# The second matrix products of two MLPs with seven block products in place of eight, in a float32 decoder trunk

## The chip, the cores and the metric

The kernel runs on one core of a Trainium2 chip. The metric is the device time of one execution in microseconds. The time before is the median of three runs, 1213.51 us (1211.22 to 1214.91). The trace comes from one further execution, recorded by the hardware profiler. Line numbers (L297) are those of the kernel before.

## The reference

The reference is a decoder trunk of two layers on 512 tokens of width 1024, in float32. Layer 1 mixes tokens with differential attention, layer 2 with an mLSTM. After each mixer stands an MLP with a squared ReLU, and both parts are added to the residual stream. A last RMSNorm ends it.

```python
def sqrelu_mlp(h, w1, w2):
    return jnp.square(jax.nn.relu(h @ w1)) @ w2
...
        h = h + mix.astype(h.dtype)
        h = h + sqrelu_mlp(rmsnorm(h, mlp_norm[layer]), mlp_w1[layer], mlp_w2[layer]).astype(h.dtype)
    return rmsnorm(h, final_norm)
```

`w1` is 1024 x 4096 and `w2` is 4096 x 1024, so that each MLP has two products of 512 x 1024 x 4096 multiply-adds. The change touches the second one, with `w2`.

## The kernel before

**Layout.** The residual stream lies transposed in SBUF: `h[k]` (k = 0 to 7) holds 128 channels by 512 tokens, two of them to a tile `h2`. A matmul takes a 128 x 128 tile of weights as its stationary operand and streams up to 512 token columns.

**Three matmuls for one product.** Float32 precision comes from splitting each operand into a high part in the format float32r and a low remainder (`split`, L423: ScalarE copies into the high part, VectorE subtracts to get the low one). A product is then high x high, high x low and low x high, three matmuls that accumulate in one PSUM bank (`mm3`, L296 to L299).

**Weights.** The host packs all weights in the order in which they are used, in units of 128 x 1024 numbers, 512 KB (`_plan`, L80). `issue` (L263) loads a unit through SyncE's DMA queue and splits it on ScalarE (L281) and VectorE (L282) into `whi` and `wlo`; raw, high and low tiles are rings of three. `unit` (L291) hands out the next unit and first issues those two ahead of it. A unit feeds 8 tiles times 3 matmuls.

**The MLP** (`mlp`, L733). The 4096 inner columns are done in two halves of 16 column tiles. For each tile of a half `ntile_mm` multiplies all 1024 input channels, ScalarE takes the ReLU out of PSUM, VectorE squares it, and a split makes `uh` and `ul` (L747 to L758). Then for each of the 8 output tiles two units of `w2` accumulate over the half's 16 inner tiles in one bank; VectorE multiplies by the squared token scale `rs2` (the RMSNorm's factor, pulled out behind the ReLU) and adds to `h[n]` (L766, L767). In the second half each finished `h[n]` becomes an operand of the next mixer at once (`operand`, L405), with its squares summed over tiles on GpSimd (`square_in`, L414 to L420). This sum over channels gives the next RMSNorm's factor by a matmul with a constant matrix (`token_scale`, `sums`).

**The tail** (`finish`, L1032). In layer 2 the last output tile is worked off in two halves of 256 tokens, 48 narrow matmuls each (L1084 to L1086), so that the final RMSNorm and the stores of the first half run beside the matmuls of the second. After the first half's matmuls `early_sums` (L1043) adds the squares of the first seven tiles into the statistic.

**What sets the order.** TensorE runs in the order in which the program is written (`manual_schedule`, L165). Small steps are woven into it by a count of matmul groups: `after(n, fn)` calls `fn` after n further ticks; `T_MLP`, `T_FIN` and others are such distances. For VectorE, ScalarE, GpSimd and the DMA queues the framework's planner orders the instructions when the program is built; each engine then runs its own queue in that order and waits on semaphores.

## Time and profile before

| | |
|---|---|
| median of three runs | 1213.51 us (1211.22 to 1214.91) |
| the profiled execution | 1211.02 us, span 1209.2 us |
| instructions | 14346, of them 5610 matmuls |
| mean granted TensorE clock | 0.992 |
| DMA | 111.15 MB moved, 92 GB/s on average |
| weight loads | 188 of 512 KB and 6 smaller or wider ones |

A page of the profile gives, for each engine, the time in which it was busy and its number of instructions. PE is TensorE's matmuls and PEld its weight loads, which overlap; DVE is VectorE, ACT ScalarE, POOL GpSimd, SP SyncE. Matmuls are pipelined: a row's duration is longer than the distance to the next one, so the cost of a matmul in a stream is read from the distance between starts. A row of a group names line, engine, operation, what is written and read, the shape and the count, then the busy time, the mean of one in ns, and the engine's idle time just before with what ended it. A row of the timeline gives start and duration in us, and in brackets the idle time before and its releaser. A line can be that of a helper: every ScalarE activation has L230.

### The profile page before, as it was taken

The numbers are of one execution on the slowest core, as the hardware profiler recorded it, in microseconds if no ns is written. First come the engines' busy times: TensorE is split into PE (matmuls) and PEld (weight loads), VectorE is DVE, ScalarE is ACT, GpSimd is POOL, SyncE is SP. The second block draws the span as 40 slices with busy tenths as digits, with TensorE's granted clock in tenths as the row PEclk, the third lists the DMA queues.
The fourth block names the chain that finished last, engine by engine and source line by source line (L and its number), as shares of the span: only waits on it lengthen the run. The fifth ranks groups of instructions, "written<-read, shape, count | busy, mean of one in ns | idle before, by whom it ended". The sixth has DMA issues, their size and how long they took to land.

```text
span 1209.2 us, 14346 instructions
## 1 busy us (share of the span) xinstructions
PE 1175.9 (97%) x5610; PEld 975.0 (81%) x5610; DVE 684.5 (57%) x1063; ACT 524.2 (43%) x845; POOL 168.7 (14%) x157
## 2 busy tenths in 40 slices
PE   8899999999999999999999899999999999999996
PEld 5778888888888888888887789878888888888885
DVE  6789897575433344434469857666544333444444
ACT  5567776454331223433344546655433122433221
POOL 4432332130000000001101312213000000000011
PEclk9999999999999999999999999999999999999998
DMA  6622222222322223232321221222232323222222
GB/s 197 197 70 70 79 79 71 76 99 87 103 89 90 102 87 104 87 103 89 98 93 64 89 69 53 70 87 87 92 100 87 104 88 103 90 91 101 87 70 70
DMA packets 33123, 111.15 MB, mean 92 GB/s; under 512 B 3967, under 2 KB 6034, under 8 KB 33056
## 3 DMA queue, kind: packets, MB, share of 16 engines
q1 hardware_dynamic: 30288, 103.38, 25.9%
q0 software_dynamic: 1648, 5.29, 1.6%
q10 hardware_dynamic: 1120, 1.57, 0.4%
q8 instruction: 44, 0.72, 0.2%
q14 instruction: 23, 0.19, 0.1%
HBM read 108.11 MB, written 4.74 MB: 93 GB/s over the span
## 4 chain that ended last, share of the span: by engine, by line
PE 84%; DVE 8%; ACT 3%; DMA 2%; issue 2%; POOL 1%; DVEq 0%; SPq 0%; ACTq 0%; POOLq 0%
PE bank L298 24%; PE bank L299 24%; PE bank L297 24%; PE bank L330 1%; PE bank L329 1%; PE bank L331 1%; DVE wlo_wlo L282 1%; DMA raw_raw<-wgt 1%; DVE tmp_tmp L827 1%; PE bank L623 1%; PE bank L624 1%; ACT kh_kh L230 1%; PE bank L656 1%; ACT whi_whi L230 1%; DVE e_e L643 0%
## 5 line engine op out<-in xcount | busy, mean ns | idle before, releaser
L282 DVE TENSOR_TENSOR wlo_wlo<-raw_raw,whi_whi 128x1024 fp32r<-128x1024 f32 (+1 forms) x194 | 243.1, 1253 | 269.2 <-ACT whi_whi L230 268.9
L230 ACT ACTIVATE whi_whi<-raw_raw 128x1024 fp32r<-128x1024 f32 (+1 forms) x194 | 203.6, 1049 | 403.4 <-PE bank L298 358.9
L299 PE MATMUL bank<-x_xh,wlo_wlo 128*128 128x512 f32 x768 | 306.0, 398 | 1.1 <-DVE wlo_wlo L282 1.1
L298 PE MATMUL bank<-x_xl,whi_whi 128*128 128x512 f32 x768 | 305.0, 397 | 1.1 <-DVE x_xl L409 1.1
L297 PE MATMUL bank<-x_xh,whi_whi 128*128 128x512 f32 x768 | 303.3, 395 | 2.0 <-ACT whi_whi L230 1.5
L299 PE MATMUL bank<-u_uh,wlo_wlo 128*128 128x512 f32 x496 | 197.1, 397 | 0.0
L298 PE MATMUL bank<-u_ul,whi_whi 128*128 128x512 f32 x496 | 196.3, 396 | 0.0
L297 PE MATMUL bank<-u_uh,whi_whi 128*128 128x512 f32 x496 | 193.7, 391 | 0.0
L297 PEld LDWEIGHTS bank<-x_xh,whi_whi 128*128 128x128 f32 x768 | 146.9, 191 | 35.3 <-ACT whi_whi L230 2.2
L298 PEld LDWEIGHTS bank<-x_xl,whi_whi 128*128 128x128 f32 x768 | 145.0, 189 | 34.3 <-DVE x_xl L409 1.8
L299 PEld LDWEIGHTS bank<-x_xh,wlo_wlo 128*128 128x128 f32 x768 | 144.9, 189 | 34.1 <-DVE wlo_wlo L282 2.1
L420 POOL TENSOR_TENSOR acc_acc<-acc_acc,tmp_tmp 128x512 f32<-128x512 f32 x34 | 53.6, 1576 | 717.8 <-ACT tmp_tmp L230 717.1
L297 PEld LDWEIGHTS bank<-u_uh,whi_whi 128*128 128x128 f32 x496 | 94.6, 191 | 22.0
L298 PEld LDWEIGHTS bank<-u_ul,whi_whi 128*128 128x128 f32 x496 | 93.1, 188 | 22.1
L299 PEld LDWEIGHTS bank<-u_uh,wlo_wlo 128*128 128x128 f32 x496 | 93.1, 188 | 20.2
L766 DVE TENSOR_TENSOR tmp_tmp<-bank,rs_rs 128x512 f32<-128x512 f32 x31 | 21.4, 692 | 107.1 <-PE bank L299 107.1
L230 ACT ACTIVATE u_uh<-tmp_tmp 128x512 fp32r<-128x512 f32 x64 | 40.4, 632 | 79.1 <-DVE tmp_tmp L754 78.9
L329 PE MATMUL bank<-whi_whi,x_xh 128*128 128x256 f32 (+1 forms) x256 | 72.7, 284 | 0.0
L330 PE MATMUL bank<-wlo_wlo,x_xh 128*128 128x256 f32 (+1 forms) x256 | 72.1, 282 | 0.0
L331 PE MATMUL bank<-whi_whi,x_xl 128*128 128x256 f32 (+1 forms) x256 | 72.0, 281 | 0.0
L424 DVE TENSOR_TENSOR u_ul<-tmp_tmp,u_uh 128x512 fp32r<-128x512 f32 x64 | 44.3, 692 | 39.1 <-ACT u_uh L230 39.1
L329 PEld LDWEIGHTS bank<-whi_whi,x_xh 128*128 128x128 f32 x256 | 48.3, 189 | 0.5
(242 smaller groups left out, 1493.3 us busy)
## 6 DMA issues: line engine op xcount, KB each, us to landing
raw_raw<-wgt SPq DMA_DIRECT2D x188, 512.0 KB, 3.5
skew<-frd POOLq DMA_DIRECT2D x8, 320.0 KB, 6.7
bias_bias<-skew POOLq DMA_DIRECT2D x8, 256.0 KB, 3.1
outT<-h SPq DMA_DIRECT2D x6, 256.0 KB, 2.3
raw_raw<-wgt SPq DMA_DIRECT2D x2, 528.0 KB, 3.6
h<-xT ACTq DMA_DIRECT2D x4, 256.0 KB, 6.8
raw_raw<-wgt SPq DMA_DIRECT2D x4, 256.0 KB, 8.7
h<-xT SPq DMA_DIRECT2D x4, 256.0 KB, 6.4
```

The costliest lines, as they stand in the source:

```text
L230: ins = nc.scalar.activation(out, x, func, **kw)
L282: vec.tensor_tensor(lo[:, c], raw[:, c], asf(hi[:, c]), op=ALU.subtract)
L297: mm(ps, whi, x[0], start=first, stop=False)
L298: mm(ps, whi, x[1], start=False, stop=False)
L299: mm(ps, wlo, x[0], start=False, stop=last)
L329: mm(ps, xh, hi[:, c], start=k == 0, stop=False)
L330: mm(ps, xh, lo[:, c], start=False, stop=False)
L331: mm(ps, xl, hi[:, c], start=False, stop=k == KT - 1)
L420: pool.tensor_tensor(acc, acc, s, op=ALU.add)
L424: (eng or vec).tensor_tensor(lo, src, asf(hi), op=ALU.subtract)
L623: mm(ps[m][:, o : o + n], q2[m][:, qs], kh[m][:, :n], start=True, stop=False)
L766: vec.tensor_tensor(y, p, rs2, op=ALU.mult)
```

## The change

The inner columns are now done in four quarters of 8 tiles. In each quarter the second product is cut into blocks: two output tiles (256 columns of `w2`) by the quarter's 1024 inner columns by 512 tokens. The weights of a block are the four pieces A11, A12, A21, A22 (512 inner columns by 128 output columns each), the hidden activations four pieces B (512 inner columns by 256 tokens each). Eight products of pieces become seven, with sums of pieces as operands:

- On the weights' side S1 = A21 + A22, S3 = A21 - A11, S2 = S1 - A11 and S4 = A12 - S2 are made on VectorE. A block's weights come as four pieces of work: `first` (two loads, and the split of A11 with A12), `sums1` (S1, S3), `half` (A22 alone) and `sums2` (S2, S4). Each MLP brings one more raw, high and low tile and a separate tile for `half`.
- On the activations' side `hidden` makes three differences of B's pieces on VectorE, and keeps seven 256-column blocks for each inner tile, all split into high and low. There are five such slots. The token scale is now applied ahead of the square, in one VectorE instruction with the ReLU, and ScalarE squares.
- `down` runs the seven products, each 4 inner tiles x 3 matmuls of 256 columns, into four PSUM banks, and assembles the block's result from them on VectorE in four additions (after ScalarE has copied the first product out of PSUM).
- In the first three quarters the assembled block is added to the residual by a DMA with an add, issued by GpSimd; in the last one by VectorE, for two tiles at once. Then follow `operand` or `square_in` for both.
- One pair of column tiles of the next quarter's first product is placed ahead of a quarter's four blocks. In the last quarter the first block takes three of the inner tiles through all products and then the fourth.
- In layer 2 the very last block stays a plain product. `finish` now works off two output tiles over one quarter, and `early_sums` follows the first of its four groups of 24 matmuls.
- The tiles of the weight rings are picked by a list of free ones, and the GpSimd DMAs' descriptor space is set to 4096.

The diff, cut to what the text speaks of:

```diff
--- before.py
+++ after.py
@@ -80,6 +80,7 @@
...
+    def pair(m, q, p, kind="pair"):
+        for n in (2 * p, 2 * p + 1):
+            units.append((m, [(8 * q + 2 * s + i, n * P, P) for i in range(2) for s in range(4)]))
+        if kind == "pair":
+            pairs.add(len(units) - 2)
...
+        for what, q, i in MLP_ORDER:
+            if what == "up":
+                for n in (8 * q + 2 * i, 8 * q + 2 * i + 1):
+                    if n >= 4:
+                        ntile(m1, n * P)
+            else:
+                pair(m2, q, i, "plain" if last and (q, i) == (3, 3) else "pair")
...
+MLP_ORDER = [("up", 0, i) for i in range(4)]
+for _q in range(4):
+    if _q < 3:
+        MLP_ORDER.append(("up", _q + 1, 0))
+    MLP_ORDER += [("down", _q, i) for i in range(4)]
+    if _q < 3:
+        MLP_ORDER += [("up", _q + 1, i) for i in range(1, 4)]
+PLAN, PAIRS = _plan()
+PIECES = []
+for _u in range(len(PLAN)):
+    if _u in PAIRS:
+        PIECES += [(kind, _u) for kind in ("first", "sums1", "half", "sums2")]
+    elif _u - 1 not in PAIRS:
+        PIECES.append(("unit", _u))
...
+    def fits():
+        kind, u = PIECES[state["next"]]
+        mine = PLAN[u][0][0] == "w"
+        def some(tag):
+            return sum((mine or all(t is not e for e in extra.get(tag, ()))) and id(t) not in live for t in ring[tag])
+        if kind == "half":
+            return id(extra["half"][0]) not in live
+        if not some("whi") or not some("wlo"):
+            return False
+        return kind not in ("unit", "first") or some("raw") > (kind == "first")
     def issue():
...
+        i = state["next"]
+        kind, u = PIECES[i]
+        assert fits()
         state["next"] += 1
...
+        if kind == "first":
+            extra["pair"] = room("raw", u), room("raw", u)
+            for i, r in enumerate(extra["pair"]):
+                nc.sync.dma_start(r[:, :1024], source(u + i))
+        r1, r2 = extra["pair"]
+        a11, a12, a21, a22 = r1[:, :512], r1[:, 512:1024], r2[:, :512], r2[:, 512:1024]
+        sums_of = extra["sums"]
+        s1, s3, s2, s4 = (sums_of[:, i * 512 : (i + 1) * 512] for i in range(4))
+        if kind == "first":
+            split(r1[:, :1024], hi[:, :1024], lo[:, :1024])
+        elif kind == "half":
+            split(a22, hi, lo)
+        elif kind == "sums1":
+            vec.tensor_tensor(s1, a21, a22, op=ALU.add)
+            vec.tensor_tensor(s3, a21, a11, op=ALU.subtract)
+            split(sums_of[:, :1024], hi[:, :1024], lo[:, :1024])
+        else:
+            vec.tensor_tensor(s2, s1, a11, op=ALU.subtract)
+            vec.tensor_tensor(s4, a12, s2, op=ALU.subtract)
+            split(sums_of[:, 1024:], hi[:, :1024], lo[:, :1024])
+            free(r1, r2)
...
         return ps
+    chains = sp.tile([P, 4 * T], F32, name="chains")
     def chain(tag):
-        return sp.tile([P, T], F32, tag=tag, name=nm(tag), bufs=1)
+        i = ("nx", "ny", "na", "sq").index(tag)
+        return chains[:, i * T : (i + 1) * T]
...
-            up = Buffers(tc, st, name="up", bufs=32)
+            up = Buffers(tc, st, name="up", bufs=1)
+            B = 256
+            slots = [tuple(up.tile([P, 7 * B], F32R, name=f"u{s}{i}") for s in "hl") for i in range(5)]
+            for tag in ("raw", "whi", "wlo"):
+                t = up.tile([P, 1024], F32 if tag == "raw" else F32R, name=f"{tag}x")
+                extra[tag] = [t]
+                ring[tag].insert(0, t)
+            extra["half"] = [up.tile([P, 512], F32R, name=f"half{s}") for s in "hl"]
+            extra["sums"] = up.tile([P, 2048], F32, name="wsums")
+            work = up.tile([P, 8 * B], F32, name="work")
+            F = chains
+            fb = F.rearrange("p (b c) -> p b c", c=B)
+            wb = work.rearrange("p (b c) -> p b c", c=B)
...
-            rs2 = scale_tile("rs2")
-            def scale():
-                rs = tmp()
-                token_scale(acc, rs)
-                act(rs2, rs, AF.Square)
-            after(T_MLP, scale)
-            for half in range(2):
...
+            def hidden(p, j, q, i):
+                m = tmp()
+                vec.scalar_tensor_tensor(m, p, 0.0, rs, op0=ALU.max, op1=ALU.mult)
+                act(fb[:, 2:8:5] if j == 0 else fb[:, 0:2], m.rearrange("p (a c) -> p a c", a=2), AF.Square)
+                if j == 0:
+                    return
+                b12 = fb[:, 7:8].to_broadcast([P, 2, B])
+                vec.tensor_tensor(fb[:, 3:5], b12, fb[:, 1:3], op=ALU.subtract)
+                vec.tensor_tensor(fb[:, 5], fb[:, 2], fb[:, 3], op=ALU.subtract)
+                vec.tensor_tensor(fb[:, 6], fb[:, 0], fb[:, 5], op=ALU.subtract)
+                hi, lo = slots[(4 * q + i) % 5]
+                split(F[:, : 7 * B], hi, lo)
+                if finish is not None and q == 3:
+                    split(F[:, 7 * B :], *spare(i))
+            PRODUCTS = (("P1", "A11", 2), ("P2", "A12", 0), ("P4", "A22", 6), ("P5", "S1", 4), ("P7", "S3", 3),
+                        ("P6", "S2", 5), ("P3", "S4", 1))
+            def down(q, i):
+                for z in list(held):
+                    done_with(z)
+                own = [take() for _ in range(4)]
+                ahead(own[-1])
+                forms = {}
+                for z, names_ in zip(own, (("A11", "A12"), ("S1", "S3"), ("A22",), ("S2", "S4"))):
+                    for j, name in enumerate(names_):
+                        forms[name] = [t[:, j * 512 : (j + 1) * 512] for t in ready[z]]
+                def more():
+                    if state["next"] <= min(own[-1] + 4, len(PIECES) - 1) and fits():
+                        issue()
+                more()
+                d, a, c, b = (bank() for _ in range(4))
...
+                       "P3": c[:, :B], "P4": c[:, B:]}
+                late = q == 3 and i == 0
+                for ks in ((0, 1, 2), (3,)) if late else ((0, 1, 2, 3),):
+                    for name, w, block in PRODUCTS:
+                        hi, lo = forms[w]
+                        for k in ks:
+                            uh, ul = slots[(4 * q + k) % 5]
+                            t = slice(block * B, (block + 1) * B)
+                            n = slice(k * P, (k + 1) * P)
+                            first = k == 0 and not (late and name in ("P7", "P6", "P3"))
+                            mm(out[name], hi[:, n], uh[:, t], start=first, stop=False, skip_group_check=late)
+                            mm(out[name], hi[:, n], ul[:, t], start=False, stop=False, skip_group_check=late)
+                            mm(out[name], lo[:, n], uh[:, t], start=False, stop=k == 3, skip_group_check=late)
+                            tick()
+                        if ks[-1] == 3:
+                            if name == "P1":
+                                act(wb[:, 7], d[:, :B], AF.Copy)
+                            last = {"P2": 0, "P7": 1, "P4": 2, "P3": 3}.get(name)
+                            if last is not None:
+                                done_with(own[last])
+                                more()
+                def two(z):
+                    return z.rearrange("p (a c) -> p a c", a=2)
+                vec.tensor_tensor(wb[:, 0:5:4], two(a), wb[:, 7:8].to_broadcast([P, 2, B]), op=ALU.add)
+                vec.tensor_tensor(wb[:, 5:7], two(b), wb[:, 4:5].to_broadcast([P, 2, B]), op=ALU.add)
+                vec.tensor_tensor(wb[:, 1:3], two(c), wb[:, 5:7], op=ALU.add)
+                vec.tensor_tensor(wb[:, 3], b[:, :B], wb[:, 6], op=ALU.add)
+                hp_ = h2[i].rearrange("p a t -> p (a t)")
+                if q < 3:
+                    nc.gpsimd.dma_start(hp_, work[:, : 4 * B], accum_op=ALU.add)
+                    return
+                vec.tensor_tensor(hp_, hp_, work[:, : 4 * B], op=ALU.add)
+                for n in (2 * i, 2 * i + 1):
+                    if g0 is not None:
                         nxt.append(operand(n, g0, nacc))
-                    elif half == 1:
+                    else:
                         if n == 0:
-                            facc = acc_tile()
-                            finish.acc = facc
+                            finish.acc = acc_tile()
                         square_in(n, finish.acc)
+            after(T_MLP, lambda: token_scale(acc, rs))
...
+            for what, q, i in MLP_ORDER:
+                if what == "up":
+                    for j in range(2):
+                        n = 2 * i + j
+                        hidden(ps[n] if q == 0 and n < 4 else ntile_mm(x), j, q, i)
+                elif finish is not None and (q, i) == (3, 3):
+                    def operands(k, t):
+                        s, j = k % 4, k // 4
+                        hi, lo = slots[(12 + s) % 5]
+                        block = (2, 7)[t] if j == 0 else t
+                        if block == 7:
+                            return spare(s)
+                        w = slice(block * B, (block + 1) * B)
...
-    def finish(hid, rs2):
-        last = KT - 1
+    def finish(operands):
+        pair = (KT - 2, KT - 1)
         acc = finish.acc
...
                 mm(s[:, :H], ones_d, sh[:, c], start=True, stop=False)
                 mm(s[:, :H], ones_d, sl[:, c], start=False, stop=False)
...
-        def tail(c, stat, wait):
-            y = tmp()[:, :H]
-            vec.tensor_tensor(y, part[:, c], rs2[:, c], op=ALU.mult)
-            vec.tensor_tensor(h[last][:, c], h[last][:, c], y, op=ALU.add)
-            s = tmp()[:, :H]
-            act(s, h[last][:, c], AF.Square)
-            vec.tensor_scalar(h[last][:, c], h[last][:, c], col(C_FN + last), -0.5, op0=ALU.mult, op1=ALU.mult)
-            after(wait, lambda: scaled(c, stat, s))
...
+        def scaled(c, stat, ss):
+            for s in ss:
+                mm(stat[:, :H], ones_df, s, start=False, stop=s is ss[-1])
             x, y, a = (chain(t)[:, :H] for t in ("nx", "ny", "na"))
...
-                    mm(part[:, c], hi[:, w], a, start=u + k == 0, stop=False)
-                    mm(part[:, c], hi[:, w], b, start=False, stop=False)
-                    mm(part[:, c], lo[:, w], a, start=False, stop=u == 1 and k == KT - 1)
+                    a, b = operands(k, i)
+                    mm(part[j][:, c], hi[:, w], a, start=k == 0, stop=False)
+                    mm(part[j][:, c], hi[:, w], b, start=False, stop=False)
+                    mm(part[j][:, c], lo[:, w], a, start=False, stop=k == KT - 1)
                     tick()
+                tail(n, c, ss[j])
+                if i == 0 and j == 0:
+                    early_sums()
             if i == 0:
-                early_sums()
-                tail(c, stat[i], T_FIN)
+                after(T_FIN, lambda c=c, ss=ss: scaled(c, stat[0], ss))
             else:
-                tail(c, stat[i], 0)
...
-    nc = _bacc.Bacc("TRN2", target_bir_lowering=False, num_devices=1)
+    nc = _bacc.Bacc("TRN2", target_bir_lowering=False, num_devices=1, dynamic_dma_scratch_size=4096)
     aps = {}
```

More of the change, by code (lines that the diff above doesn't have):

```diff
@@ L296, in mm3, with ahead, done_with, take @@
+    used = iter(range(len(PIECES)))
+    held = []
+    def ahead(i):
+        while state["next"] <= min(i, len(PIECES) - 1):
+            issue()
+    def done_with(i):
+        held.remove(i)
+        free(*ready.pop(i))
+    def take():
+        i = next(used)
+        held.append(i)
+        return i
+    def unit(n=2, keep=False):
+        if not keep:
+            for i in list(held):
+                done_with(i)
+        i = take()
+        ahead(i + n)
+        return ready[i]
     def mm3(ps, whi, wlo, x, first, last):
@@ L746, in mlp @@
[L746 to L768 removed]
+            rs = scale_tile("rs2")
@@ L775, in mlp @@
+            for tag in ("raw", "whi", "wlo"):
+                (t,) = extra.pop(tag)
+                ring[tag] = [r for r in ring[tag] if r is not t]
             return nxt, nacc
```

140 lines of the change are left out of this document (72 added, 68 removed).

## The prediction

> **What bounds the kernel now.** I read the page's busy table first, then its busy slices, then busy time by stage, then the groups by shape inside one stage, then single rows at the two places where the change shortens a cover.
>
> ```profile
> span 1209.2 us, 14346 instructions
> PE 1175.9 (97%) x5610; PEld 975.0 (81%) x5610; DVE 684.5 (57%) x1063; ACT 524.2 (43%) x845; POOL 168.7 (14%) x157
> PE 84%; DVE 8%; ACT 3%; DMA 2%; issue 2%; POOL 1%; DVEq 0%; SPq 0%; ACTq 0%; POOLq 0%
> ```
>
> TensorE is busy for 97% of the span and carries 84% of the chain that ended last. The profiled execution took 1211.02 us, 1.8 more than its span, and lies 2.5 us under the median of the three runs (1213.51). Those runs spread over 0.3%, which is about what a measurement of this kernel can tell from no change.
>
> ```profile
> core 0: us, PE busy (x) PEld busy (x) DVE busy (x) ACT busy (x) POOL busy (x), PEclk, DMA share, GB/s
> 826.00:1184.40 358.40, 358.40 (x1546) 291.39 (x1545) 152.53 (x173) 113.75 (x145) 13.66 (x9) 1.00 0.28 92
> 1184.40:1209.20 24.80, 13.44 (x105) 12.55 (x103) 13.38 (x22) 4.71 (x10) 5.08 (x3) 0.84 0.25 85
> ```
>
> ```profile
> 1184.42 0.28 PE L1084 MATMUL bank<-u_uh,whi_whi 128*128 128x256 f32 x1
> ...
> 1190.12 0.28 PE L1046 MATMUL bank<-sh_sh,ones_d 128*128 128x256 f32 x1
> ```
>
> The first row is the second layer's MLP up to its last column tile: TensorE is never idle there (358.40 of 358.40 us) at full granted clock, while VectorE is busy 43% and ScalarE 32%. So in this stage a matmul removed is time removed, as long as nobody else becomes late. Two prices follow. A 512-column matmul: 358.40 us / 1546 = 0.2318 us. A 256-column matmul: the last two rows bracket the 48 matmuls of lines 1084 to 1086 on the first token half, in the same pattern the change uses (high x high, high x low, low x high), so 5.70 us / 48 = 0.1188 us. Two narrow ones cost 0.2375 against 0.2318 for a wide one, 2.5% more per column.
>
> **Term 1, TensorE's work.** One block of the second product is two column tiles by one quarter (8 row tiles) of the inner columns. Before: 2 x 8 x 3 = 48 wide matmuls, 11.13 us. After: 7 products x 4 row tiles x 3 = 84 narrow ones, 9.98 us. Layer 1 has 16 blocks: 768 x 0.2318 = 178.0 becomes 1344 x 0.1188 = 159.7, or -18.3. Layer 2 has 720 wide and 96 narrow ones (166.9 + 11.4 = 178.3); it gets 15 blocks and a last plain one of 96 narrow matmuls, 1356 x 0.1188 = 161.1, or -17.2. Together **-35.5 us**. The first product's matmuls stay as they are.
>
> Here the Trainium skill speaks against the change: "TensorE: Matmul & The Clock Gate", section "LDWEIGHTS (loading the stationary operand)", puts a weight load at columns / 1.2 ns, so about 107 ns for 128 columns, and its Part 3 says that loads overlap running matmuls only in another row group. By that, 107 + 107 = 214 ns per narrow matmul, the block would grow to 84 x 0.214 = 18.0 us. The narrow matmuls of this trace start 0.1188 us apart, each with a load of its own, so the trace does not agree.
>
> **Term 2, VectorE and ScalarE in the blocks.** What is added has no price on TensorE unless it makes weights or banks late. The groups by shape in a stretch of second products give the prices:
>
> ```profile
> L282 DVE TENSOR_TENSOR wlo_wlo<-raw_raw,whi_whi 128x1024 fp32r<-128x1024 f32 x17 | 20.8, 1222 | 35.7 <-ACT whi_whi L230 35.7
> L298 PEld LDWEIGHTS bank<-u_ul,whi_whi 128*128 128x128 f32 x102 | 19.2, 188 | 4.5
> L230 ACT ACTIVATE whi_whi<-raw_raw 128x1024 fp32r<-128x1024 f32 x16 | 17.0, 1061 | 67.1 <-PE bank L298 67.1
> L766 DVE TENSOR_TENSOR tmp_tmp<-bank,rs_rs 128x512 f32<-128x512 f32 x7 | 4.8, 692 | 24.3 <-PE bank L299 24.3
> L754 DVE TENSOR_TENSOR tmp_tmp<-tmp_tmp 128x512 f32<-128x512 f32 x2 | 1.4, 685 | 0.0
> L230 ACT ACTIVATE u_uh<-tmp_tmp 128x512 fp32r<-128x512 f32 x2 | 1.3, 632 | 2.8 <-DVE tmp_tmp L754 2.8
> ```
>
> ```profile
> 1190.32 0.42 DVE L1054 TENSOR_TENSOR tmp_tmp<-bank,rs_rs 128x256 f32<-128x256 f32 x1 [0.51 <-PE bank L1086]
> ```
>
> VectorE per second-product block: three 1024-wide splits (A11 with A12, S1 with S3, S2 with S4) 3 x 1.222, the half split of A22 0.69, four 512-wide sums 4 x 0.685, the assembly of four results 3 x 0.692 + 0.42: **9.6 us in 9.98**. Before it was 2 x 1.222 plus two evictions. ScalarE: 3 x 1.061 + 0.632 + 0.42 = 4.2 us. VectorE per first-product block (two column tiles, 11.13 us on TensorE): two splits 2.44, two evictions 1.38, three subtractions 0.685 + 2 x 0.42, and a 1792-wide split, by width 1.75 x 1.222 = 2.14: 7.5 us. So VectorE goes from idle half of the time to 17.1 of 21.1 us, yet stays under TensorE in both kinds of block.
>
> Its queue is not free of gaps: the low half of each split waits for ScalarE's high half, and those of the sums can't start before the sums. The written order would leave it idle about 1.1 us at each of the two sum pieces, 11.8 us a block. But every piece of block b+1 is written while block b runs. Reckoned from the start of b: the first split ends by 4 us and is due at 10; the first sums end by 8, due at 14.3 (three of seven products into b+1); the second sums, whose tile product five frees at 7.1, end by 10 to 12, due at 17. So each has 5 to 7 us in hand, and TensorE doesn't see the gaps. I take 0 for each of the eight quads (four quarters in two layers); the bound is 2 us a quad, and below 0 there is nothing, since TensorE had no idle time here to give back.
>
> The 24 adds into the residual that go through GpSimd as accumulating DMAs lie off every chain until the third quarter's sum is read, some 40 us later; but each reads `work`, which the next block's assembly overwrites after its sixth product, 8.55 us into the block, or 7.3 us after the issue at about 1.2.
>
> ```profile
> raw_raw<-wgt SPq DMA_DIRECT2D x188, 512.0 KB, 3.5
> skew<-frd POOLq DMA_DIRECT2D x8, 320.0 KB, 6.7
> ```
>
> The trace has no accumulating DMA. Its nearest rows are 3.5 us for a plain 512 KB load and 6.7 for GpSimd's copies issued eight at a time; 5 to 7 us fits into 7.3, so I take 0.
>
> The Trainium skill, "DMA: Bandwidth & Descriptors", section "Anatomy of one DMA — SWDGE (gpsimd) path", gives about 2.0 us + bytes/436e3 for a plain transfer from GpSimd, by estimate 3.2 us for 512 KB; no run here shows an accumulating one, and the sum would be the same.
>
> **Term 3, the tail of the second layer.** Here an exposed chain appears. `finish` multiplies the square sums of the finished tiles into `stat` (lines 1046 and 1047) between its matmuls. The chain for it before:
>
> ```profile
> 1184.62 0.69 DVE L766 TENSOR_TENSOR tmp_tmp<-bank,rs_rs 128x512 f32<-128x512 f32 x1 [3.42 <-PE bank L299]
> ...
> 1186.13 0.63 ACT L230 ACTIVATE tmp_tmp<-h 128x512 f32<-128x512 f32 x1 [6.19 <-DVE h L767]
> 1188.46 0.63 ACT L230 ACTIVATE sh_sh<-acc_acc 128x512 fp32r<-128x512 f32 x1 [1.69 <-POOL acc_acc L420]
> ...
> 1186.90 1.52 POOL L420 TENSOR_TENSOR acc_acc<-acc_acc,tmp_tmp 128x512 f32<-128x512 f32 x1 [9.69 <-ACT tmp_tmp L230]
> ...
> 1189.12 0.69 DVE L424 TENSOR_TENSOR sl_sl<-acc_acc,sh_sh 128x512 fp32r<-128x512 f32 x1 [1.84 <-ACT sh_sh L230]
> ```
>
> It ended at 1189.81, 5.4 us after the last wide matmul's successor at 1184.42, and TensorE came to line 1046 at 1190.12: hidden by 48 narrow matmuls. After the change two column tiles end together, and `early_sums` stands behind only the first 24 matmuls, 2.85 us. The chain from the end of block (3,2): 0.2, the one assembly step that needs the last product 0.69, the 1024-wide residual add 1.22, two squares 0.63 + 0.63, two GpSimd adds of 1.52 of which the first runs beside the second square, the split 0.63 + 0.69. With the handoffs GpSimd starts at 2.9 and ends at 5.95; the high half is there at 6.6, the low at 7.3. TensorE stands from 2.85 until 7.3: **+4.4 us** (0 if GpSimd and ScalarE overlap better than the row, 6 with VectorE's leftovers ahead). TensorE is in written order, so nothing fills this. The dropped multiply by the scale at the very end (0.42) about pays for one more stat matmul.
>
> **Term 4, the step into the second mixer.** The same doubling sits on a chain that already ends exactly on time:
>
> ```profile
> 611.68 0.69 DVE L766 TENSOR_TENSOR tmp_tmp<-bank,rs_rs 128x512 f32<-128x512 f32 x1 [3.35 <-PE bank L299]
> 612.29 0.42 DVE L789 CAST sel<-tmp_tmp 128x512 fp32r<-128x512 f32 x1
> 612.62 0.68 DVE L767 TENSOR_TENSOR h<-h,tmp_tmp 128x512 f32<-128x512 f32 x1
> ...
> 617.62 0.68 DVE L424 TENSOR_TENSOR sl_sl<-acc_acc,sh_sh 128x512 fp32r<-128x512 f32 x1
> ...
> 618.35 0.50 PE L432 MATMUL bank<-sl_sl,ones_d 128*128 128x512 f32 x1
> ```
>
> `sl` was ready at 618.30 and its matmul ran at 618.35: no slack. With two tiles arriving together and four ScalarE steps (two high halves, two squares) before the second GpSimd add, I reckon 7.4 to 8.3 us instead of 6.8; and in this last quad VectorE also does the residual add and two operands in each block (9.6 + 1.2 + 1.4 = 12.2 against 9.98), so it enters behind by a few us. I take **+2.0 us**, between 0 and 6.
>
> **The sum.** -35.5 + 0 + 4.4 + 2.0 = -29.1. Against the profiled execution 1211.0 - 29.1 = 1181.9; the median lies 2.5 higher, so 1184.
>
> **The rivals.** *Both chains hidden*: TensorE sees only term 1, 1213.5 - 35.5 = 1178. For it: the planner that orders VectorE and ScalarE may put the needed steps first. Against: line 432 above had no slack even with one tile.
>
> *VectorE short in the blocks*: 9.6 of 9.98 us leaves little, and the low halves wait for ScalarE. If each of the eight quads costs 1 to 2.2 us, 1192 to 1202. Against it: 5 to 7 us in hand per piece and a first product of 7.5 in 11.1 between quads.
>
> *Slower by order*: at the start of a quad the pieces `half` and `sums2` are written behind the eviction of the last first-product tile, a chain of eviction 0.7, square 0.6, subtractions 0.7 + 0.8, and a 1792-wide split of 1.75 x 1.061 = 1.9 and 2.1, 6.8 us from that tile's end, and product three wants `half` at 2.85. Run in written order, `half` is ready at about 8, so TensorE stands some 5.2 us in each of eight quads: +42, or 1226. It decides from 29.1 / 8 = 3.6 us a quad. Against it speak the rows of term 4: line 789 belongs to the next stage, written far later, and sits on VectorE between lines 766 and 767. So queues are ordered by readiness, not as written.
>
> *The accumulating DMA as a new wait*: VectorE's assembly waits for `work`; if a DMA takes L, a block can't be shorter than L + 2.7. At 12 us the lag is 4.7 a block; three in a quad make 14, 7 are in hand, 7 are lost in each of six quads: 42, again 1226. Up to 9 us it costs nothing; slower from about 11. Against it: twice the 3.5 us row is 7.
>
> *Loads not hidden*: if the 188 ns load (line 298) bounded a narrow matmul, a block would take 84 x 0.188 = 15.8, +4.7 in 31 blocks, about +145: 1358. The 0.1188 spacing excludes it almost. Beside it stands the Trainium skill's rule above, that a load doesn't overlap in the same row group.
>
> **How the numbers follow.** The forecast 0.60, both hidden 0.10, VectorE short 0.15, slower by order 0.08, accumulating DMA 0.06, loads 0.01. Faster by over 0.3% are the first three: 0.85. Of the order and DMA cases 0.03 end within 0.3%, 0.12 slower. The range goes from 1174 (both chains hidden, 1178, less 4 for the spread of the runs) to 1202 (the upper end of VectorE short in the blocks, or the forecast with both chains at their upper bounds, 6 more, and 1.5 us a quad).
>
> **What would show it.** Right: TensorE's matmul count up by 1116, narrow ones 0.119 us apart, 9.98 us a block; no TensorE idle inside quads; one gap near 4.4 us ahead of the early square sums waiting for ScalarE or VectorE, one near 2 ahead of the mixer's token sums; VectorE busy over 75% in the MLPs; accumulating DMAs landing within 8 us. Wrong: narrow matmuls further apart than 0.125; gaps whose releaser is a weight's low half or `half` at the third product; VectorE standing on a DMA before the assembly.

## The result, and the profile after

The changed kernel takes 1195.0 us (median of four runs, 1193.95 to 1195.75). The kernel before, timed beside it, takes 1213.24 (1211.22 to 1214.91). The ratio is 0.985, with a 95% interval of 0.9832 to 0.9868, so the change saves 18 us where 29 were forecast. The profiled execution took 1194.34 us. The page of the profile:

```profile
span 1192.3 us, 17221 instructions
PE 1147.5 (96%) x6730; PEld 1011.2 (85%) x6730; DVE 919.9 (77%) x1387; ACT 603.0 (51%) x909; POOL 189.2 (16%) x180
...
PE 78%; DVE 14%; ACT 3%; issue 3%; DMA 2%; POOL 1%; DVEq 0%; SPq 0%; POOLq 0%; ACTq 0%
```

TensorE has 1120 matmuls more and is busy 28 us less. But its share of the chain that ended last falls from 84% to 78%, and VectorE's rises from 8% to 14%: in some places the kernel now waits for VectorE. Where these are, the busy time by stage shows. The stages are: the first mixer; layer 1's MLP; the first product of the second mixer, with the token sums behind it; the rest of that mixer; layer 2's MLP up to `finish`; the tail. Columns are the stretch, its length, busy time and count of each engine, then the granted clock, the DMA engines' busy share and GB/s. First the kernel before (its tail stands in the prediction), then the one after:

```profile
0.00:262.30 262.30, 247.95 (x1330) 209.19 (x1331) 209.47 (x448) 172.57 (x349) 91.81 (x98) 0.99 0.32 104
262.30:611.50 349.20, 349.20 (x1507) 284.01 (x1506) 143.96 (x168) 112.58 (x145) 9.82 (x7) 1.00 0.29 96
611.50:624.00 12.50, 12.50 (x100) 12.24 (x99) 9.84 (x19) 5.89 (x8) 1.27 (x1) 1.00 0.28 85
624.00:846.30 222.30, 214.70 (x1117) 182.03 (x1117) 164.73 (x246) 123.01 (x200) 53.51 (x43) 0.98 0.23 74
846.30:1184.40 338.10, 338.10 (x1458) 274.95 (x1458) 143.16 (x163) 105.48 (x134) 7.23 (x5) 1.00 0.27 91
```

```profile
0.00:261.50 261.50, 248.88 (x1329) 210.43 (x1330) 210.32 (x448) 173.48 (x350) 91.55 (x98) 0.99 0.34 107
261.50:593.60 332.10, 330.85 (x2083) 299.20 (x2082) 258.75 (x325) 147.31 (x168) 16.58 (x15) 1.00 0.41 115
593.60:615.70 22.10, 14.97 (x101) 14.45 (x100) 18.75 (x26) 9.39 (x14) 6.76 (x5) 0.77 0.30 97
615.70:838.70 223.00, 215.22 (x1119) 182.13 (x1118) 166.04 (x248) 123.87 (x201) 52.96 (x43) 0.98 0.25 76
838.70:1159.00 320.30, 320.30 (x1998) 289.09 (x1997) 247.92 (x317) 142.98 (x163) 13.63 (x14) 1.00 0.40 114
1159.00:1192.30 33.30, 17.27 (x110) 15.87 (x108) 18.14 (x28) 5.95 (x13) 7.74 (x6) 0.77 0.19 63
```

The two MLPs gain 17.1 and 17.8 us, 34.9 together. The two short stages behind them give 18.1 back: the mixer's first product goes from 12.5 to 22.1 us (+9.6), the tail from 24.8 to 33.3 (+8.5). With -0.8 and +0.7 in the mixers the sum is -16.9, the difference of the spans. In both short stages the granted clock has fallen to 0.77, from 1.00 and 0.84. TensorE's waits there, of the table of waits:

```profile
PE bank L432 <- DVE work L939: 5.7, 1, 5.7
PE bank L1249 <- ACT sh_zeros L254: 5.1, 1, 5.1
...
PE bank L432 <- DVE work L937: 1.4, 1, 1.4
...
PE bank L924 <- DVE wlox L528: 1.3, 1, 1.3
```

Lines are those of the changed kernel: L432 is the mixer's first product, L1249 the early square sums, L924 a matmul of `down`. The last row is the only wait that TensorE has in either MLP up to its last matmul; it stands in layer 1's last quarter, at 587.98.

**The step into the mixer.** The last block's last matmul runs at 593.44. VectorE, from the timeline:

```profile
593.45 1.21 DVE L945 TENSOR_TENSOR h<-h,work 128x1024 f32<-128x1024 f32 x1
594.79 0.69 DVE L937 TENSOR_TENSOR work<-bank,work 128x512 f32<-128x512 f32 x1
595.40 1.22 DVE L528 TENSOR_TENSOR wlo<-raw,whi 128x1024 fp32r<-128x1024 f32 x1
596.53 3.94 DVE L513 SCALAR_TENSOR_TENSOR x_xl<-h,colt,x_xh 128x512 fp32r<-128x512 f32 x2
600.40 0.68 DVE L938 TENSOR_TENSOR work<-bank,work 128x512 f32<-128x512 f32 x1
601.11 0.69 DVE L939 TENSOR_TENSOR work<-bank,work 128x512 f32<-128x512 f32 x1
```

The addition of line 939, which reads a finished bank, runs 7.4 us after the end of the products. VectorE stands on nothing in these rows; it is behind. The row of 595.40 even splits a weight of the mixer ahead of the operands; no run here tries another order of VectorE's queue. And VectorE is slowed: the two operands of line 513 take 3.94 us, while GpSimd adds squares (line 524) from 596.08 to 597.74 and from 598.64 to 599.92. The tile `x_xl` alone, minimum/median/maximum of one instruction in ns, after and then before:

```profile
L513 DVE SCALAR_TENSOR_TENSOR x_xl<-h,colt,x_xh x8: 740/1250/2268, 571.7 to 605.5; 128x512 fp32r<-128x512 f32 x8
```

```profile
L409 DVE SCALAR_TENSOR_TENSOR x_xl<-h,colt,x_xh x5: 743/746/750, 569.6 to 614.1; 128x512 fp32r<-128x512 f32 x5
```

**The tail.** `finish` begins at 1159.05. The chain of the squares:

```profile
1161.55 1.22 DVE L945 TENSOR_TENSOR h<-h,work 128x1024 f32<-128x1024 f32 x1
```

```profile
1162.80 1.46 ACT L254 ACTIVATE tmp_tmp<-h 128x512 f32<-128x512 f32 x3 [4.46 <-DVE h L945]
```

```profile
1163.57 2.90 POOL L524 TENSOR_TENSOR acc_acc<-acc_acc,tmp_tmp 128x512 f32<-128x512 f32 x2 [2.63 <-ACT tmp_tmp L254]
```

```profile
1167.17 0.69 DVE L528 TENSOR_TENSOR sl_sl<-acc_acc,sh_zeros 128x512 fp32r<-128x512 f32 x1 [0.55 <-ACT sh_zeros L254]
```

```profile
1167.19 0.58 PE L1249 MATMUL bank<-sh_zeros,ones_d 128*128 128x256 f32 x1 [5.12 <-ACT sh_zeros L254]
```

It ends at 1167.86, 8.8 us after block (3,2), where 7.3 were reckoned: the residual addition starts at 1161.55 and not at about 1160, because VectorE had leftovers. TensorE stands for 5.1 us.

**The clock behind the waits.** Stretches of the changed kernel; the number behind the counts of the five engines is the granted clock:

```profile
581.00:593.60 12.60, 11.35 (x96) 11.14 (x95) 12.60 (x15) 6.55 (x9) 3.83 (x2) 1.00 0.23 61
596.50:606.80 10.30, 4.94 (x22) 4.94 (x23) 10.20 (x16) 2.94 (x6) 4.71 (x4) 0.50 0.28 90
...
1166.60:1173.50 6.90, 6.17 (x27) 5.87 (x28) 0.72 (x2) 0.54 (x1) 0.00 (x0) 0.51 0.00 0
```

In the first row VectorE is busy for all of 12.60 us. By its timeline it has had no idle time since 561.45, the end of the last quarter's first block: that is where it falls behind. In the other two TensorE has half its clock, for 10.3 and 6.9 us, beginning within a wait. Whether that costs anything is a question of what else is late there; the experiments below take the two places apart.

### The profile page after: what moved, and what is told of

It is laid out like the page before. It is cut to its first block, busy times and chain, and to the rows that moved or that the text cites. A ratio compares the mean times of both kernels' runs of the same rounds, so it can differ in the third digit from the quotient of the medians.

```text
span 1192.3 us, 17221 instructions
## 1 busy us (share of the span) xinstructions
PE 1147.5 (96%) x6730; PEld 1011.2 (85%) x6730; DVE 919.9 (77%) x1387; ACT 603.0 (51%) x909; POOL 189.2 (16%) x180
## 3 DMA queue, kind: packets, MB, share of 16 engines
q10 hardware_dynamic: 1120, 1.57, 0.4%
## 4 chain that ended last, share of the span: by engine, by line
PE 78%; DVE 14%; ACT 3%; issue 3%; DMA 2%; POOL 1%; DVEq 0%; SPq 0%; POOLq 0%; ACTq 0%
PE bank L401 15%; PE bank L402 15%; PE bank L400 15%; PE bank L923 7%; PE bank L924 7%; PE bank L922 7%; DVE wlo L528 2%; PE bank L432 2%; PE bank L433 1%; PE bank L434 1%; DVE tmp_tmp L1030 1%; DMA raw<-wgt 1%; DVE x_xl L513 1%; PE bank L730 1%; ACT whi L254 1%
## 5 line engine op out<-in xcount | busy, mean ns | idle before, releaser
L402 PE MATMUL bank<-x_xh,wlo 128*128 128x512 f32 x640 | 255.4, 399 | 1.3 <-DVE wlo L528 1.3
L401 PE MATMUL bank<-x_xl,whi 128*128 128x512 f32 x640 | 254.8, 398 | 1.0 <-DVE x_xl L513 1.0
L400 PE MATMUL bank<-x_xh,whi 128*128 128x512 f32 x640 | 254.0, 397 | 1.4 <-ACT whi L254 1.4
L254 ACT ACTIVATE whi<-raw 128x1024 fp32r<-128x1024 f32 (+2 forms) x128 | 133.4, 1042 | 120.9 <-PE bank L923 48.1
L528 DVE TENSOR_TENSOR wlo<-raw,whi 128x1024 fp32r<-128x1024 f32 (+2 forms) x128 | 161.9, 1265 | 35.2 <-ACT whi L254 34.6
L922 PE MATMUL bank<-uh,whi 128*128 128x256 f32 x560 | 157.9, 282 | 0.0
L924 PE MATMUL bank<-uh,wlo 128*128 128x256 f32 x560 | 157.8, 282 | 0.0
L923 PE MATMUL bank<-ul,whi 128*128 128x256 f32 x560 | 157.8, 282 | 0.0
L400 PEld LDWEIGHTS bank<-x_xh,whi 128*128 128x128 f32 x640 | 122.8, 192 | 28.8 <-ACT whi L254 2.1
L402 PEld LDWEIGHTS bank<-x_xh,wlo 128*128 128x128 f32 x640 | 121.1, 189 | 29.3 <-DVE wlo L528 2.4
L401 PEld LDWEIGHTS bank<-x_xl,whi 128*128 128x128 f32 x640 | 121.5, 190 | 28.3 <-DVE x_xl L513 1.4
L924 PEld LDWEIGHTS bank<-uh,wlo 128*128 128x128 f32 x560 | 105.8, 189 | 0.0
L432 PE MATMUL bank<-whi,x_xh 128*128 128x256 f32 (+1 forms) x256 | 73.9, 289 | 7.1 <-DVE work L939 5.7
```

The costliest lines, as they stand in the source:

```text
L254: ins = nc.scalar.activation(out, x, func, **kw)
L400: mm(ps, whi, x[0], start=first, stop=False)
L401: mm(ps, whi, x[1], start=False, stop=False)
L402: mm(ps, wlo, x[0], start=False, stop=last)
L432: mm(ps, xh, hi[:, c], start=k == 0, stop=False)
L528: (eng or vec).tensor_tensor(lo, src, asf(hi), op=ALU.subtract)
```

## The experiments

**Theory A:** the saving on TensorE arrives in full, and it is given back only at the two seams, the steps out of the MLPs: at the mixer because VectorE is late, at the tail because the chain of squares is exposed; half clock adds to it. **Theory B:** at the mixer only the order of the PSUM banks is at fault. **Rival C:** part of the saving is lost inside the blocks, to VectorE or to the accumulating DMAs. Medians below stand beside runs of the kernel before on the same chip: 1210.03 for e1, e2, e3 and e5; 1210.97 for a0, e4, e8 and e10; 1211.55 for e6, e9, e11 and e12. Stage lengths are those of one profiled execution each. In runs whose edit leaves the stage alone, the mixer's first product takes 21.9 to 22.7 us from its first matmul to the end of its last one (22.15 in the trace above), and the tail 32.0 to 33.3; smaller differences show nothing. The changed kernel was run again in the second group:

**a0_after.** No edit. 

> The changed kernel once more, beside the next three on one chip, since the kernel before ran at 1210.0 in the first set of experiments and at 1213.2 with the changed kernel. Both theories: 1190 to 1196, the same stage lengths as in the first trace within 1 us (22 us for the mixer's first product, 33 us for the tail).

1194.91 us, ratio 0.9867 (0.9848 to 0.9885). The stages agree with those above within 0.1 us, but for the first mixer, which takes 263.6 us instead of 261.5: that much single executions differ there, and more (260.2 to 264.7 in all traces).

**e1_banks.** The mixer's product takes its bank from the ring that is free first.

```diff
-            banks(mm=3, sc=2, ac=3)
+            banks(ac=3, mm=3, sc=2)
```

> The changed kernel with one line of the mLSTM's bank table in another order, so that its first product takes the four PSUM banks that have been free longest, not three that the last block of the MLP still holds. Theory A (VectorE is late): VectorE enters the mixer some 8 us behind, and the bank is only the first thing that TensorE meets; TensorE goes through the first row tiles at once and then stands 7 to 10 us ahead of the token sums, whose squares come off the same late queue. Time 1193 to 1197, the same as the changed kernel's 1195. Rival B (the banks alone): the 7.1 us of waits and the half clock after them go, 1185 to 1188.

1197.89 us, ratio 0.989 (0.9875 to 0.9905). The wait at line 432 is gone, and in its place stands:

```profile
PE bank L535 <- ACT sh_sh L254: 9.6, 2, 9.1
```

TensorE does the product early and then waits 9.1 us for the token sums, whose chain goes through VectorE and GpSimd too. The stage takes 23.9 us instead of 22.2. Theory B falls: the bank was only where the lag was met first.

**e2_late_sums.** The early square sums come ten ticks later, so that 48 matmuls and some of the second half's cover their chain.

```diff
                 tail(n, c, ss[j])
-                if i == 0 and j == 0:
-                    early_sums()
             if i == 0:
-                after(T_FIN, lambda c=c, ss=ss: scaled(c, stat[0], ss))
+                after(10, early_sums)
+                after(11, lambda c=c, ss=ss: scaled(c, stat[0], ss))
```

> The changed kernel with the early square sums of the tail put 10 matmul groups behind the first token half instead of after its first tile (and the first half's statistic one group later). Theory A (the wait costs twice, itself and the half clock that the profile grants for some 7 us after it): the gap of 5.4 us goes and the tail runs at full clock; the tail of 33.3 us from the last block's end falls to 25 to 26, time 1186 to 1188. Rival B (only the wait counts, the clock record is no cost): 1189.5 to 1191. Rival C (the first half's normalization, now later, delays the end as much): 1193 to 1196.

1188.75 us, ratio 0.9818 (0.9804 to 0.9833). The wait is gone and the tail takes 26.7 us, 6.6 less; the other stages stay within 0.7 us. So of the tail's +8.5 us, 6.6 are the place of `early_sums` (at least 5.3 by the shortest tail that was left alone), 1.9 are left. The time lies between the forecasts of theory A and rival B.

**e3_filler.** 20 matmuls of 512 columns, whose results nobody reads, stand ahead of the early square sums. TensorE then has 1.0 us of idle time left ahead of the sums and keeps its clock.

```diff
...
                 if i == 0 and j == 0:
+                    spill = bank()
+                    for _ in range(20):
+                        mm(spill, hi[:, :P], fill(), start=True, stop=True)
                     early_sums()
```

> The changed kernel with 20 matmuls of 512 columns that nobody reads (about 4.6 us) ahead of the tail's early square sums, into a bank of their own, so that TensorE works through the wait; the wait itself stays. Theory A: no half clock is granted after it, and the 72 narrow matmuls behind it take 8.6 us in place of about 11.5; time 1191 to 1193. Rival B (the record is not the array's pace, or the drop has another cause): 1194 to 1197.

1193.09 us, ratio 0.9849 (0.9834 to 0.9864). The tail of this kernel:

```profile
1160.50:1191.40 30.90, 19.16 (x130) 16.91 (x128) 18.12 (x28) 5.96 (x13) 7.72 (x6) 0.90 0.20 68
```

The chain comes no earlier (the high half's matmul starts 8.2 us after `finish` begins, 8.1 in the changed kernel), but the tail is 2.4 us shorter (33.3 to 30.9), and 1.1 shorter than the shortest of the tails left alone. With useless work in the gap the tail gets shorter, so half clock has a price there, between 1.1 and 2.4 us. That the whole kernel is faster the times don't show: the ratio is that of the changed kernel (0.985 and 0.9867). The rest of what e2 gains, about 4 us, goes with the wait itself.

One of the tails left alone fits this. In e1 the tail takes 32.2 us, and more of its half clock falls into the wait:

```profile
1169.10:1175.90 6.80, 3.62 (x15) 3.33 (x16) 3.16 (x3) 0.73 (x2) 2.24 (x2) 0.50 0.00 0
```

TensorE works 3.62 us at half clock there and 6.17 in the changed kernel. At half pace that is 1.3 us less lost, by estimate; the tail is 1.1 shorter.

**e5_plain_last.** Layer 1's last block stays a plain product too, 96 narrow matmuls as in layer 2, so that VectorE has fewer steps there and each tile is done with one addition.

```diff
-                pair(m2, q, i, "plain" if last and (q, i) == (3, 3) else "pair")
+                pair(m2, q, i, "plain" if (q, i) == (3, 3) else "pair")
...
-                elif finish is not None and (q, i) == (3, 3):
+                elif (q, i) == (3, 3):
...
+                    for j, n in enumerate((KT - 2, KT - 1)):
...
+                                mm(ps[:, o], hi[:, w], uh, start=k == 0, stop=False)
+                                mm(ps[:, o], hi[:, w], ul, start=False, stop=False)
+                                mm(ps[:, o], lo[:, w], uh, start=False, stop=k == KT - 1)
+                                tick()
+                        vec.tensor_tensor(h[n], ps, h[n], op=ALU.add)
...
```

> The changed kernel with the last block of the first MLP done as a plain product too, 96 narrow matmuls with the two output tiles one after the other (TensorE 1.4 us more, VectorE about 6.5 us less in that block). Theory A (VectorE's lag in the last quad makes the wait at the step into the mixer): the 7.1 us of waits shrink to under 2 and no half clock follows; time 1186 to 1189. Rival B (banks): the waits shrink as well, since fewer banks are held, but then the run with the other bank order has gained as much. Rival C (the chain of squares through GpSimd, as in the prediction, whatever VectorE's lag): 1193 to 1197.

1188.98 us, ratio 0.9819 (0.9798 to 0.9839). The block has 12 matmuls more (1.4 us), and the MLP takes no longer, since the wait of 1.25 us in its last quarter is gone. The mixer's first product falls from 22.2 to 16.8 us. The wait there:

```profile
PE bank L432 <- DVE h L988: 2.7, 1, 2.7
```

The wait was expected to fall below 2 us with no half clock behind it; 2.7 stay, and the stage's granted clock is 0.90.

**e6_acc_vec.** In the last quarter of both MLPs VectorE adds the squares, not GpSimd. That gives VectorE more to do and takes its neighbour away.

```diff
...
-            pool.tensor_tensor(acc, acc, s, op=ALU.add)
+            adds[0].tensor_tensor(acc, acc, s, op=ALU.add)
...
+                adds[0] = vec
                 for n in (2 * i, 2 * i + 1):
...
```

> The changed kernel with the adds that sum the squares moved from GpSimd to VectorE in the last quarter of both MLPs. In the changed kernel's trace two operand steps of VectorE take 3.94 us instead of 1.41 while GpSimd adds beside them. Theory A (GpSimd's adds slow VectorE, and lengthen both exposed chains): the mixer's first product falls from 22.2 to 18 to 20.5 us and the tail from 33.3 to 28 to 32; 3 to 8 us less than the changed kernel. Rival (VectorE is the one that is late, and six to eight more adds of 0.69 make it later): no gain or up to 3 us more.

1189.78 us, ratio 0.9822 (0.9793 to 0.9852). The mixer's product takes 19.6 us, the tail 31.0: 4.9 us are gained at the two seams although VectorE has more work, and `x_xl` is back at its old price:

```profile
L513 DVE SCALAR_TENSOR_TENSOR x_xl<-h,colt,x_xh x8: 742/744/747, 570.7 to 602.6; 128x512 fp32r<-128x512 f32 x8
```

The waits at both seams stay, shorter (4.4 at line 432, 3.8 at the early sums). So GpSimd's adds explain some of VectorE's lag, not all.

**e4_vec_load.** VectorE gets four more additions of 512 columns in each of the 24 blocks of the first three quarters; nobody reads their results.

```diff
                 if q < 3:
+                    for _ in range(4):
+                        vec.tensor_tensor(wb[:, 5:7], wb[:, 5:7], wb[:, 5:7], op=ALU.add)
                     nc.gpsimd.dma_start(hp_, work[:, : 4 * B], accum_op=ALU.add)
```

> The changed kernel with four more 512-wide VectorE additions (2.4 to 2.7 us) whose results nobody reads, in each of the 24 blocks of the first three quarters, behind the assembly. VectorE then has 12.0 to 12.3 us of work in a block of 9.98. Theory A (each piece of weights has 5 to 7 us in hand): the lag of 2.0 to 2.3 us a block reaches 8 to 9 at the end of a quad, TensorE loses at most 1 to 3 us in each of six quads, time within 4 to 15 us of the changed kernel. Rival (VectorE's queue already bounds the blocks): all of the 58 to 64 us show.

1196.63 us, ratio 0.9882 (0.986 to 0.9903), 1.7 above the changed kernel, with intervals that overlap. Its MLPs, by its own stages:

```profile
262.40:594.50 332.10, 330.85 (x2083) 299.20 (x2082) 287.70 (x373) 146.88 (x168) 16.57 (x15) 1.00 0.41 116
840.20:1160.70 320.50, 320.41 (x1998) 289.11 (x1997) 276.90 (x365) 142.55 (x163) 13.67 (x14) 1.00 0.40 114
```

VectorE is busy 29 us longer in each, 86 to 87% of the time, and the stages grow by 0.0 and 0.2 us. Even theory A had expected some loss; there was more room than it thought. Rival C falls for VectorE in the first three quarters.

**e8_vec_add.** The residual additions of the first three quarters run on VectorE in place of the 24 accumulating DMAs.

```diff
+                vec.tensor_tensor(hp_, hp_, work[:, : 4 * B], op=ALU.add)
                 if q < 3:
-                    nc.gpsimd.dma_start(hp_, work[:, : 4 * B], accum_op=ALU.add)
                     return
-                vec.tensor_tensor(hp_, hp_, work[:, : 4 * B], op=ALU.add)
```

> The changed kernel with the residual add of the first three quarters on VectorE too, in place of the 24 accumulating DMAs: 1.22 us more for VectorE a block, no wait of the assembly for the DMA that reads its tile. Theory A: VectorE has 10.8 us of work in 9.98, a lag of 3.4 us a quad that the 5 to 7 us in hand cover; time within 1.5 us of the changed kernel. Rival B (the DMA's waits, 16 us of VectorE's idle time in the trace, reach TensorE): 3 to 8 us faster. Rival C (VectorE short): 10 to 29 us slower.

1196.25 us, ratio 0.9874 (0.9855 to 0.9892), 1.3 above the changed kernel with overlapping intervals; both MLPs take what they took (332.0 and 320.4). The DMAs cost TensorE nothing, and the additions would have cost nothing either.

**e9_before_early.** The kernel before, with one thing of the change alone: the early square sums stand behind 24 of the 48 matmuls of the first token half.

```diff
                     mm(part[:, c], lo[:, w], a, start=False, stop=u == 1 and k == KT - 1)
                     tick()
+                if i == 0 and u == 0:
+                    early_sums()
             if i == 0:
-                early_sums()
                 tail(c, stat[i], T_FIN)
```

> The kernel before with its early square sums after 24 of the first half's 48 narrow matmuls, so that TensorE waits for the chain that ended 5.4 us after the last wide matmul: a gap of about 2.5 us. If a gap costs only itself, the tail grows from 24.75 to 27.2 us and the time by 2.5. If a gap of this length also brings the half clock, it grows to 28 to 31. In the changed kernel the two gaps with a half clock were 5.1 and 5.7 us long, and one of 1.5 us had none.

1215.59 us, ratio 1.0035 (1.002 to 1.005): 4 us slower. The tail takes 29.3 us, 4.5 more than before and within what was expected if half clock follows. Two stretches of 3.4 us in its tail:

```profile
1185.49:1188.90 3.41, 1.36 (x10) 1.15 (x10) 0.69 (x1) 0.63 (x1) 1.01 (x1) 1.00 0.00 0
1188.90:1192.31 3.41, 3.41 (x19) 3.41 (x18) 0.00 (x0) 0.00 (x0) 0.00 (x0) 0.50 0.00 0
```

TensorE is idle for 2.05 us in the first and has half clock throughout the second, where it never idles: some 1.7 us lost, almost as much as the wait. So such a loss needs no seven products; a cover that is half as long does it.

**e11_mixer_filler.** 28 matmuls whose results nobody reads stand ahead of the mixer's first product, to keep the clock up there as e3 does in the tail.

```diff
+            spill = bank("sc")
+            for _ in range(28):
+                mm(spill, ones_d, x[0]()[0], start=True, stop=True)
             psv = vpair_mm(x, 264)
```

> The changed kernel with 28 matmuls of 512 columns that nobody reads (about 6.5 us) ahead of the mixer's first product, in a bank of their own, so that TensorE works through most of the wait. Theory A (an idle stretch of about 6 us brings the half clock): no half clock after it, the product's stage falls from 22.2 to 19 to 20 us, the time by 2 to 3. Rival (the clock has nothing to do with the idle stretch): stage 22 us or more.

1197.25 us, ratio 0.9871 (0.985 to 0.9891): no gain, against theory A, which expected that the half clock costs here too. Its product from the end of the fillers on, at a clock of 1.00, and a row of its timeline where TensorE still stands:

```profile
603.27:618.71 15.44, 13.07 (x100) 12.29 (x99) 12.65 (x23) 5.86 (x9) 3.27 (x2) 1.00 0.16 48
```

```profile
612.40 0.49 PE L535 MATMUL bank<-sh_sh,ones_d 128*128 128x512 f32 x1 [1.21 <-ACT sh_sh L254]
```

Fillers and product take 21.97 us together (from 596.74 on), as long as the stage without them (22.15). In the changed kernel the low half of the token sums is ready at 609.83 and its first matmul starts at 610.00: the slow matmuls ahead of it end just when the late chain does. At this seam the half clock is covered; the chain that comes off the late VectorE sets the time.

**e10_all.** Layer 1's plain last block, the late sums and the order of the banks together (e5, e2 and e1).

> The changed kernel with the plain last block in the first MLP, the late square sums in the tail, and the mixer's first product in the banks that have been free longest. Theory A (VectorE's lag first, then the bank): with the lag gone the bank order counts, the mixer's first product falls from 22.2 us to 13 to 14.5, the tail from 33.3 to 26.7; 15 us less than the changed kernel beside it. Rival (the parts don't add up, a wait comes back at the token sums): 10 to 12 us less.

1180.61 us (1179.87 to 1183.23), ratio 0.9751 (0.973 to 0.9771), 14.3 below the changed kernel on the same chip. The two seams:

```profile
594.10:608.70 14.60, 12.91 (x101) 12.35 (x100) 10.44 (x20) 4.72 (x7) 4.89 (x3) 1.00 0.24 71
...
1151.50:1178.20 26.70, 14.30 (x110) 13.19 (x108) 18.01 (x28) 5.96 (x13) 7.69 (x6) 0.82 0.23 79
```

The gains add up: the tail's 6.6, the mixer's 5.4 of e5, and 2.2 more there (16.8 to 14.6). The order of the banks, worth nothing alone (e1), is worth something once the chain behind it is shorter.

**e12_all_acc_vec.** e10 with e6 on top.

> The version with all three repairs (1180.6), and the squares' adds on VectorE in the last quarter. Theory A: the mixer's first product 14.6 falls to 12.6 to 13.5, the tail stays near 26.7; 1178.5 to 1180. Rival: 1180 to 1183, since the waits left there are short.

1181.01 us, ratio 0.9736 (0.9712 to 0.976), the same as e10 within the intervals. The mixer's product takes 12.52 us, as in the kernel before (12.51): that seam is whole again. The tail takes 27.2. What this gains at the mixer does not show in the median, which lies in the rival's range: in these two traces the first mixer takes 1.8 us longer and the tail 0.6, and the first of these is within what single executions differ.

## Why the prediction was off by 11 us

**Term 1 and term 2 held.** TensorE's work was to fall by 35.5 us and the blocks were to lose nothing; the MLP stages fell by 34.9, and the one wait of 1.25 us in layer 1 is a loss within them. Its releaser is a weight's low half, one of the signs named for being wrong; it came once. In layer 1's first quarter the blocks' narrow matmuls begin at 309.73 and the next quarter's wide ones at 349.76: 40.03 us for four blocks, 10.01 for one, 9.98 forecast. The row of line 922 shows 0.0 us of idle time for 560 matmuls:

```profile
L922 PE MATMUL bank<-uh,whi 128*128 128x256 f32 x560 | 157.9, 282 | 0.0
```

So narrow matmuls with a load each keep their 0.119 us, and *loads not hidden* is out. *Slower by order* is out with the same row. *The accumulating DMA* is out twice: the page gives 5.8 us to landing, and e8 without it is not faster.

```profile
h<-work POOLq DMA_DIRECT2D x24, 512.0 KB, 5.8
```

Another of the signs named does show, among VectorE's waits:

```profile
DVE work L937 <- DMA h<-work: 16.0, 10, 2.1
```

VectorE does stand on these DMAs ahead of the assembly, for 16.0 us in ten places. In e8 these waits are gone and the time is not less, so they don't reach TensorE.

*VectorE short in the blocks* gave 1192 to 1202, and the time lies there, but not for that reason: e4 puts 2.8 us more on VectorE in each of 24 blocks, and TensorE does not notice. VectorE is short in one place only, the last quarter of each MLP, where the residual additions and the next operands come on top.

**Term 4 was mis-sized: +9.6 us, where +2.0 was taken and 6 was the upper end.** The step that failed is "so it enters behind by a few us. I take +2.0 us". The working had 12.2 us of VectorE work per block against 9.98, but did not carry that through the quarter's blocks (three of them make 6.7 us, by estimate), and priced the squares' chain as if VectorE and GpSimd ran at the prices of the kernel before. It reckoned the low half of the sums 7.4 to 8.3 us after the products, and a few more for the lag; it was ready at 609.83, 16.1 us after them. The runs show both: e6, without GpSimd beside it, takes 2.6 us off, e5, with less VectorE work, 5.4; the parts overlap and were not separated to the last microsecond. Half clock comes with it but costs nothing of its own here (e11).

**Term 3 was mis-sized: +8.5 us, where +4.4 was taken.** The mechanism is the one described, `early_sums` behind too short a cover. The wait was 5.1 instead of 4.4, since VectorE arrived with leftovers. What the step left out altogether is that TensorE runs at half clock behind such a wait: 1.1 to 2.4 us by e3. And 1.9 us stay even without the wait (e2).

Together: the terms of the seams were 11.7 us too small (9.6 + 8.5 against 2.0 + 4.4), the MLPs 0.6 too good; that is the 12.4 between 1181.9 and the profiled 1194.3, but for 0.1.

That the time lies within 1174 to 1202 is in part luck. Both seams went beyond the upper ends given for them (6 and 6); with these alone the forecast reaches 1189.6. The rest of the range was an allowance for VectorE short in the blocks, a loss that hardly came.

## What to carry to other kernels

When a change speeds up a stage that one engine fills, price the seams behind it anew: the engine that had slack inside the stage arrives late at its end, and the work that covered a chain there has become shorter. In such a seam look at which chain ends last before moving anything: the order of the banks alone gained nothing here (e1), and the same order beside a shorter chain did (e10). Leaving the last block of a stage in the old form, putting exposed sums behind more work and then changing the bank order won back 14 of the 18 us lost (e10).

## What the runs showed of the hardware

- Idle time of TensorE is followed by a stretch at half clock. The granted clock changes in steps of 3.41 us. Over the 14 traces of this case (their first steps aside), a step at full clock in which TensorE's recorded matmuls leave 1.9 us or more idle was followed by half clock, and one that leaves under 1.5 us was not; in between both occur (1.77 us, from 593.09 to 596.50 in the changed kernel, sufficed). Full clock came back after a step with at most 0.57 us idle. In e9 2.05 us of idle time, in two pieces, were enough; the half clock then lasted 3.4 us although TensorE was never idle in it. Behind the longer waits of the changed kernel it lasted 6.9 and 10.3 us, two and three times as much. The Trainium skill, "TensorE: Matmul & The Clock Gate", "What's actually happening", has the clock fall to half after at least one idle window of about 3.4 us, and return after one busy window. The granted 0.50 and the length of the stretches agree; the idle time needed does not, since 2.05 us sufficed.
- A VectorE instruction with two operands from SBUF took up to three times as long beside a GpSimd addition: `x_xl` 0.74 to 2.27 us in the changed kernel, 0.742 to 0.747 in e6, where GpSimd adds nothing there. The Trainium skill, "SBUF — State Buffer", "SBUF: two separate sides", says that such an instruction and a GpSimd one lock each other out of a port pair that they share; this trace agrees in kind.
